# Holding a step until its input is there by the estimate: a re-recorded order for a two-layer hybrid block

## The chip, the cores and the metric

One core of a Trainium2 chip runs the whole program. The metric is the device time of one execution in microseconds (us); what is compared is the median of several runs.

## What is computed

The reference is a block of DEPTH 2 over 256 tokens `x` and 256 context tokens, width 1024, in float32:

```python
def hybrid_layer(x, ctx, sc, sc_ctx, ...):
    shift, scale, gate = jnp.split((sc @ w_ada + b_ada)[:, None, :], 3, axis=-1)
    h = rmsnorm(x, norm_w) * (1.0 + scale) + shift
    aq, ak, av, ag, ao, az, bq, bk, bv, bz, cu, cz, mg = split_cols(h @ w_in)
    ...
    h_a, h_a_c = mlstm_mixer(qa, ka, va, ga, qa_c, ka_c, va_c, ga_c)   # branch A, 4 heads, both directions
    o_b = attend_blocked(qb, ..., lam)                                 # branch B, differential attention
    y_c = fourier_mix(cu) * jax.nn.silu(cz)                            # branch C, fft2
    x = x + gate * merge(y_a, y_b, y_c, mg, w_a_out, w_b_out, w_c_out, w_out)
```

Layer 0 computes tokens and context, layer 1 only the tokens' queries; `merge` gates each branch's output product by a sigmoid and multiplies the sum by `w_out`.

## The kernel before

**Tiles.** Every matmul is made of three products of parts: a float32 operand is split into a hi part (fp32r) and a lo part, its remainder, and hi·hi, hi·lo and lo·hi are summed in PSUM. A weight piece of 512 rows by 256 columns is loaded into `raw`, ScalarE (ACT) copies it to `wh`, and VectorE (DVE) subtracts to make `wl` (`emit_split`, L506, three buffers each). The normalized input, feature-major, is held as `hTh` and `hTl` for the whole layer.

**Two streams of work.** The main stream is the large products with the weights, in chunks of 256 columns (`fm_chunk` L561, `tm_chunk` L587) into the three PSUM banks `pm`. The order of the chunks is a string per layer (ORDER0, ORDER1: A heads, B groups, C groups, merges M, out W). Everything else is side work: the gates of branch A with their scans (`gates_side` L673), the heads (`a_side` L819), attention (`b_side` L986), the Fourier products (`c_side` L1143), the norm of layer 1; it uses five PSUM banks `ps`. Side work is written as generators. After each main step `tick` (L630) continues them, up to about 500 ns of TensorE's time (SIDE_NS) at once, if the time that the generator named by `when(...)` (L186: its tiles written, a bank free, 400 ns on top) has come on an estimated clock.

**What sets the order.** Each engine executes its instructions in the order in which the program emits them. `Clocks` (L91) keeps an estimated time per engine: `book` adds an estimated cost for each instruction, and `Paced` (L127) does so on every call of DVE, ACT, GpSimd (POOL) and SyncE. The estimates only place instructions; a wait on the chip is by semaphores. In this version a step that consists of an ACT and a DVE instruction is emitted whole:

```python
    def split(src, hi, lo, scale=None):
        if scale is None:
            scalar.copy(hi, src)
            vector.tensor_tensor(lo, src, f32(hi), op=ALU.subtract)
```

So DVE's subtract stands in DVE's order right where the ACT copy was emitted, and DVE waits there for ACT.

**The start.** The scale and shift of the norm come from products of `w_ada`, a quarter of the features at a time (`quarter`, L1369). For each quarter: 32 small products of `adaw` on TensorE, `adar` on DVE, 8 tiny products, two `ab` on DVE, then ACT and DVE scale `xT`, ACT casts it to `hTh`, DVE subtracts to `hTl`, for the context tokens and then for the others. Between quarters the first products of head A0 run (table START), on `wh`, `wl` made by `split_to` (L522).

**Names.** In branch A: `gpad` gates before the scans, `lfm`, `Rc`, `Rx`, `at` the scans' tiles, transposed on TensorE by `first` (the identity) and turned into `acol`, `ecol`; `qkh`, `qkl` a head's q and k; `S` their products; `H` the head's output; `Ga` the output gate. In branch B: `kT`, `qT`, `W`, `vt`, and `O`, whose squares `os` go through POOL. L161 is the line of all DVE, ACT and POOL instructions, L232 that of all matmuls, L236 that of transposes.

Of the kernel before, what the change touches and what calls it, by code (L numbers as in the profile page):

```python
# [27 lines left out]
NGEN = 28  # L28
MAINB = 3
# [12 lines left out]
ORDER1 = "A0 B0 A1 B1 A2 A3 C0 B2 B3 M0 C1 C2 C3 M1 M2 W0"  # L42
AHEAD = ((0, 1, 1), (1, 1, 0))
# [47 lines left out]
class Clocks:  # L91
    """When each engine gets to what is emitted, estimated, to place the side work among the main products."""

    def __init__(self):
        self.t = {"pe": 0.0, "dve": 0.0, "act": 0.0, "pool": 0.0, "sync": 0.0}
        self.wrote, self.read, self.ring = {}, {}, {}

    def book(self, engine, outs, ins, cost, tail):
        """an instruction of engine: names of tiles written and read, time held, time until the result is seen"""
# [15 lines left out]

    def rotate(self, tag, bufs, name):
        """the tile called name takes the place of the one bufs before it"""
# [9 lines left out]
class Paced:  # L127
    """An engine whose instructions are booked as they are emitted."""
# [38 lines left out]
def hybrid_kernel(ctx: ExitStack, tc: tile.TileContext, t):  # L167
# [37 lines left out]
    def gen_pair(shape, name):  # L205
        """hi and lo parts, in one slot where they fit"""
# [8 lines left out]
    def ps_main():  # L215
        b = pp.tile([128, 512], F32, tag="pm", name=nm("pm"), bufs=MAINB)
        est.rotate("pm", MAINB, b.name)
        return b

    def ps_side():  # L220
        b = pp.tile([128, 512], F32, tag="ps", name=nm("ps"), bufs=SIDEB)
# [6 lines left out]
    def mm(o, a, b, start, stop):  # L228
        n = int(np.prod(b.shape[1:]))
        ins = [v.name for v in (a, b) if v.name not in ("hTh", "hTl")]  # L230
        est.book("pe", [o.name], ins, max(n * 0.4167 + 2.5, 27) * (4 if b.dtype == F32 else 1) / (128 // o.shape[0]), 160)
        nc.tensor.matmul(out=o, lhsT=a, rhs=b, start=start, stop=stop)  # L232

    def transpose(o, a, idn):
        est.book("pe", [o.name], [a.name], 112, 160)
        nc.tensor.transpose(o, a, idn)  # L236

    def split(src, hi, lo, scale=None):
        if scale is None:
            scalar.copy(hi, src)  # L240
            vector.tensor_tensor(lo, src, f32(hi), op=ALU.subtract)
        else:
            scalar.activation(out=hi, in_=src, func=ACTF.Copy, scale=scale)
            vector.scalar_tensor_tensor(lo, src, scale, f32(hi), op0=ALU.mult, op1=ALU.subtract)

    # ------------------------------------------------------------- constants
# [73 lines left out]
    def rstd_of(ss, n, shape):  # L320
        """(ss / n + eps) ** -0.5 on GpSimd, in place; returns the time at which it is done"""
# [4 lines left out]
    # ------------------------------------------------------------- per-layer small parameters  # L326
# [46 lines left out]
    def ada_rows(l, piece, dma):  # L373
        """w_ada of 512 columns"""
# [8 lines left out]
    def ada_mm(raws, brow, dst):  # L383
        """sc @ w_ada + b_ada: partitions 32 g + stream hold four partial sums"""
# [13 lines left out]
    def ada_finish(l, pc, ks=slice(0, 8)):  # L398
        """pc: shift and scale of some blocks of features"""
# [9 lines left out]
    def ada_gen(l, pieces):  # L409
        """shift and scale columns (pieces 0..3) as a side generator"""  # L410
# [34 lines left out]
    # ------------------------------------------------------------- norm -> feature-major h  # L445
# [3 lines left out]
    def norm_stats(tiles):  # L449
        """normalized copies of some token tiles"""  # L450
# [10 lines left out]
    def norm_apply(l, i, src, base):  # L461
        """src: the normalized transposed blocks base .. base + 3 of token tile i; returns the closing step"""
# [23 lines left out]
    # ------------------------------------------------------------- weight pieces  # L486
# [4 lines left out]
    def emit_raw(i):  # L491
        r = wp.tile([128, 4, 256 + GATES], F32, tag="raw", name=nm("raw"), bufs=RAWB)
# [13 lines left out]
    def emit_split(i):  # L506
        r = made[i]
        n = r.shape[2]
        h = wp.tile([128, 4, 256 + GATES], F32R, tag="wh", name=nm("wh"), bufs=WB)
# [35 lines left out]
    def wcols(w, *cols, form=None):  # L545
        """two pieces of some columns; even features before odd ones along the columns or in pairs of row blocks"""
# [4 lines left out]
    # ------------------------------------------------------------- main-stream products  # L551
# [9 lines left out]
    def fm_chunk(rhs, evac, ntok, bank=ps_main, step=4):  # L561
        """two 128-column blocks of W, feature-major: out[block][128 cols, tokens]"""
# [24 lines left out]
    def tm_chunk(lhs, tiles, evac, single=False, step=4):  # L587
        """256 columns of W, token-major: out[pair][128 tokens, 2, 256]"""
# [24 lines left out]
    # ------------------------------------------------------------- side machinery  # L613
# [4 lines left out]
    def launch(g):  # L618
        rec = {"g": g, "due": 0.0, "done": False}
        side.append(rec)  # L620
        return rec
# [8 lines left out]
    def tick():  # L630
        pe0 = clocks["pe"]
        for rec in list(side[:ACTIVE]):
# [12 lines left out]

    def hrhs(t0, n):
# [7 lines left out]
    # ============================================================= one layer  # L654
# [841 lines left out]
```

## Time and profile before

| what | value |
|---|---|
| runs | 1522.76 us median of 3 (1522.49 to 1524.54) |
| profiled execution | span 1521.1 us from first to last instruction |
| TensorE (PE) | 1499.1 us busy, 99% |
| VectorE (DVE) | 971.5 us, 64% |
| ScalarE (ACT) | 735.0 us, 48% |
| GpSimd (POOL) | 145.7 us, 10% |
| granted TensorE clock | 1.00, mean over the span |

The profile shows one execution, and its span is the time given for it; the median of the runs is 1.66 us above that span. TensorE's matmuls are pipelined: a row's duration (0.28 us for 256 columns) is longer than the distance to the next row's start, so the cadence is read from starts. "Idle" in a bracket is the time between the modelled end of one instruction and the start of the next.

### The profile page before, as it was taken

Reading aid. Unit: us, or ns where it says so; the run is one execution under the profiler, and the core shown is the slowest. Engines: PE = TensorE matmul, PEld = TensorE weight load, DVE = VectorE, ACT = ScalarE, POOL = GpSimd, SP = SyncE. Lnnn points to the kernel's source line nnn. Section 1 sums busy time; section 2 is a strip of 40 time slices with the busy share of each in tenths; the row PEclk is TensorE's granted clock in tenths of the full one; section 3 lists DMA queues with packets and bytes.
Section 4 is the critical chain, followed back from the end, with each engine's and each line's share of the span. In section 5 each row is a group of like instructions: output and inputs, shape, how many; then the busy total and the mean of one; then the engine's idle time right before and its main releaser. Section 6 shows DMA issues by size and latency. Waiting matters only on the chain.

```text
span 1521.1 us, 25867 instructions
## 1 busy us (share of the span) xinstructions
PE 1499.1 (99%) x10410; PEld 1350.8 (89%) x10410; DVE 971.5 (64%) x1833; ACT 735.0 (48%) x1384; POOL 145.7 (10%) x193
## 2 busy tenths in 40 slices
PE   6999999999999999999999999999999999999999
PEld 4888889999998987897786789999999999999998
DVE  3447666677677586436664367677687666977765
ACT  4443556544544545334432235545557554656443
POOL 4001000020100010001024001001020011000200
PEclk9999999999999999999999999999999999999999
DMA  9524333332222222223249337544344523545754
GB/s 310 167 84 127 87 94 105 105 97 70 75 67 69 70 84 70 84 84 97 70 144 337 78 112 228 139 131 133 115 111 118 167 84 109 169 139 153 256 162 151
DMA packets 181611, 192.07 MB, mean 126 GB/s; under 512 B 9818, under 2 KB 174612, under 8 KB 181492
## 3 DMA queue, kind: packets, MB, share of 16 engines
q1 hardware_dynamic: 170080, 159.93, 35.6%
q0 software_dynamic: 7936, 27.27, 5.9%
q10 hardware_dynamic: 3476, 3.23, 0.7%
q8 instruction: 81, 1.33, 0.4%
q14 instruction: 38, 0.31, 0.1%
HBM read 188.23 MB, written 2.17 MB: 125 GB/s over the span
## 4 chain that ended last, share of the span: by engine, by line
PE 92%; DVE 3%; SPq 2%; issue 1%; ACT 1%; DMA 1%; ACTq 0%; DVEq 0%
PE pm L232 76%; PE ps L232 13%; PE ps L236 3%; SPq L161 2%; DVE wl L161 1%; DVE Rx L161 1%; DMA raw<-in_w_in_dram 0%; DVE Rc L161 0%; DMA prow<-in_a_norm_w_dram 0%; DVE lfm L161 0%; DVE at L161 0%; ACT lse L161 0%; DVE Ga L161 0%; ACT wh L161 0%; DVE ntmp L161 0%
## 5 line engine op out<-in xcount | busy, mean ns | idle before, releaser
L161 DVE TENSOR_TENSOR wl<-raw,wh 128x1024 fp32r<-128x1024 f32 x280 | 340.9, 1223 | 193.4 <-ACT wh L161 192.8
L161 ACT CAST wh<-raw 128x1024 fp32r<-128x1024 f32 x280 | 293.6, 1054 | 169.0 <-PE pm L232 135.0
L232 PE MATMUL pm<-hTh,wh 128*128 128x256 f32 (+1 forms) x1008 | 349.0, 346 | 0.0
L232 PE MATMUL pm<-hTl,wh 128*128 128x256 f32 (+1 forms) x1008 | 342.8, 340 | 0.0
L232 PE MATMUL pm<-hTh,wl 128*128 128x256 f32 (+1 forms) x1008 | 342.4, 340 | 0.0
L232 PE MATMUL pm<-wh,hTh 128*128 128x256 f32 (+1 forms) x1152 | 329.8, 286 | 1.5 <-DVE Ga L161 0.8
L232 PE MATMUL pm<-wl,hTh 128*128 128x256 f32 (+1 forms) x1152 | 324.1, 281 | 0.7 <-DVE wl L161 0.7
L232 PE MATMUL pm<-wh,hTl 128*128 128x256 f32 (+1 forms) x1152 | 324.2, 281 | 0.3 <-DVE hTl L161 0.2
L232 PEld LDWEIGHTS pm<-wh,hTh 128*128 128x128 f32 x1152 | 217.3, 189 | 10.4 <-issue 5.5
L232 PEld LDWEIGHTS pm<-wl,hTh 128*128 128x128 f32 x1152 | 216.9, 188 | 2.1 <-DVE wl L161 1.0
L232 PEld LDWEIGHTS pm<-wh,hTl 128*128 128x128 f32 x1152 | 217.5, 189 | 0.7 <-DVE hTl L161 0.7
L232 PEld LDWEIGHTS pm<-hTh,wh 128*128 128x128 f32 x1008 | 189.7, 188 | 30.8 <-issue 9.9
L232 PEld LDWEIGHTS pm<-hTh,wl 128*128 128x128 f32 x1008 | 189.5, 188 | 23.3
L232 PEld LDWEIGHTS pm<-hTl,wh 128*128 128x128 f32 x1008 | 189.7, 188 | 19.0
L232 PE MATMUL pm<-y,wh 128*128 128x512 f32 (+1 forms) x768 | 192.7, 342 | 0.0
L232 PEld LDWEIGHTS pm<-y,wh 128*128 128x128 f32 x768 | 128.9, 188 | 18.3 <-issue 2.6
L232 PE MATMUL pm<-y,wl 128*128 128x512 f32 (+1 forms) x384 | 129.4, 337 | 0.0
L161 ACT ACTIVATE Pt<-ps,mx,qsc 128x512 f32<-128x512 f32 (+1 forms) x96 | 67.1, 706 | 27.7 <-DVE mx L161 22.0
L232 PEld LDWEIGHTS pm<-y,wl 128*128 128x128 f32 x384 | 72.2, 188 | 8.6
L232 PE MATMUL pm<-wh,yf 128*128 128x256 f32 x384 | 73.0, 287 | 0.0
L232 PEld LDWEIGHTS pm<-wh,yf 128*128 128x128 f32 x384 | 59.9, 188 | 0.3
L161 DVE TENSOR_REDUCE mx<-ps 128x1 f32<-128x512 f32 (+1 forms) x96 | 53.0, 593 | 4.3 <-PE ps L232 4.2
(243 smaller groups left out, 1969.8 us busy)
## 6 DMA issues: line engine op xcount, KB each, us to landing
raw<-in_w_in_dram SPq DMA_DIRECT2D x192, 512.0 KB, 3.7
adaw<-in_w_ada_dram POOLq DMA_DIRECT2D x32, 512.0 KB, 7.1
raw<-in_w_out_dram SPq DMA_DIRECT2D x24, 512.0 KB, 4.5
adaw<-in_w_ada_dram SPq DMA_DIRECT2D x16, 512.0 KB, 8.5
raw<-in_w_in_dram SPq DMA_DIRECT2D x32, 256.0 KB, 3.3
raw<-in_w_a_out_dram SPq DMA_DIRECT2D x16, 512.0 KB, 3.4
raw<-in_w_c_out_dram SPq DMA_DIRECT2D x32, 256.0 KB, 3.4
raw<-in_w_b_out_dram SPq DMA_DIRECT2D x16, 512.0 KB, 3.8
```

The costliest lines, as they stand in the source:

```text
L161: return f(*a, **k)
L232: nc.tensor.matmul(out=o, lhsT=a, rhs=b, start=start, stop=stop)
L236: nc.tensor.transpose(o, a, idn)
```

## The change

- `Clocks` gets a list of held steps. `later(src, tiles, fn)` puts a step there with a due time, the estimated time at which its input `src` is written. `elapse` emits due steps ahead of the next DVE or TensorE instruction; `settle` emits a held step when an instruction touches one of its tiles; `clear` does so before a buffer of a ring is reused.
- Held are: the lo part of every `split` (so every `wl`, `hTl` of the start, `qkl`, and the like); in `a_side` the copy of `S` with its masked form `Sd`, and the normalizing `rr`, `H`; the second step of the output gates; in `b_side` the three steps from a product to `O` and its square; in `c_side` the whole split of `T`.
- A matmul's estimated cost becomes its cadence: `max((n * 0.4453 + 4) * (4 if F32), 105)`, times the shares of rows and columns used, where it was `max(n * 0.4167 + 2.5, 27)` times 4 and divided by the row groups; a transpose's 109 where it was 112.
- NGEN, the slots of the general pool, goes from 28 to 30, and the scratch of dynamic DMAs is set to 8192. FLIP_H, FLIP_O, FLIP_K, FLIP_W are False, and the code under them is not reached.

The number of instructions of each engine stays the same. The core of the diff:

```diff
+    def later(self, due, tiles, fn):
+        names = {v.name for v in tiles}
+        for n in names:
+            self.read.setdefault(n, {})["later"] = due + 1200
+        self.held.insert(self.held.index(self.at[-1]) if self.at else len(self.held), (due, names, fn))
...
+    def settle(self, names):
+        while q := next((q for q in self.before() if q[1] & names), None):
+            self.emit_held(q)
+
+    def elapse(self):
+        while not self.at and (q := next((q for q in self.held if q[0] <= max(self.t["pe"], self.t["dve"])), None)):
+            self.emit_held(q)
...
         def call(*a, **k):
+            if self.key == "dve":
+                self.clocks.elapse()
+            self.clocks.settle({v.name for v in list(a) + list(k.values()) if hasattr(v, "shape") and hasattr(v, "name")})
...
     def when(*tiles, banks=1):
...
-        return max([0.0] + [est.wrote[v.name][1] for v in tiles if v.name in est.wrote] + [est.last(n) for n in old]) + READY_NS
+        held = [est.read[v.name]["later"] for v in tiles if "later" in est.read.get(v.name, {})]
+        return max([0.0] + held + [est.wrote[v.name][1] for v in tiles if v.name in est.wrote] +
+                   [est.last(n) for n in old]) + READY_NS
...
     def mm(o, a, b, start, stop):
+        est.elapse()
+        est.settle({o.name, a.name, b.name})
...
-        est.book("pe", [o.name], ins, max(n * 0.4167 + 2.5, 27) * (4 if b.dtype == F32 else 1) / (128 // o.shape[0]), 160)
+        est.book("pe", [o.name], ins, max((n * 0.4453 + 4) * (4 if b.dtype == F32 else 1), 105) * o.shape[0] / 128 * a.shape[0] / 128, 160)
...
     def split(src, hi, lo, scale=None):
+
         if scale is None:
             scalar.copy(hi, src)
-            vector.tensor_tensor(lo, src, f32(hi), op=ALU.subtract)
+            later(hi, (src, lo), lambda: vector.tensor_tensor(lo, src, f32(hi), op=ALU.subtract))
```

Three places of the order follow; names carry buffer numbers, and line 208 of the changed kernel answers to L161, 285 to L232, 291 to L236.

**VectorE in the start**, quarters 0 and 1, from `adar` of quarter 0 on. `wl_66` and `wl_73` are the lo parts of the first two weight pieces. Before:

```order
L161 TENSOR_TENSOR adar_61_246<-ps_57_216,brow_42_163 128x512
L161 TENSOR_TENSOR wl_66_260<-raw_26_127,wh_65_259 128x4x256
L161 COPY ab_71_279<-ps_67_263 128x4
L161 SCALAR_TENSOR_TENSOR ab_71_279<-ps_67_263,pcol_15_105 128x4
L161 TENSOR_SCALAR xT_58_225<-xT_58_225,ab_71_279 128x256
L161 TENSOR_TENSOR hTl_109<-xT_58_225,hTh_108 128x2x256
L161 TENSOR_SCALAR xT_58_225<-xT_58_225,ab_71_279 128x256
L161 TENSOR_TENSOR hTl_109<-xT_58_225,hTh_108 128x2x256
L161 TENSOR_TENSOR wl_73_295<-raw_31_137,wh_72_294 128x4x256
L161 TENSOR_TENSOR adar_80_334<-ps_79_317,brow_42_163 128x512
L161 COPY ab_71_279<-ps_82_349 128x4
L161 SCALAR_TENSOR_TENSOR ab_71_279<-ps_82_349,pcol_15_105 128x4
```

And in the changed kernel, from the second `ab` of quarter 0 on:

```order
L208 SCALAR_TENSOR_TENSOR ab_71_278<-ps_67_262,pcol_15_105 128x4
L208 TENSOR_SCALAR xT_58_225<-xT_58_225,ab_71_278 128x256
L208 TENSOR_TENSOR hTl_109<-xT_58_225,hTh_108 128x2x256
L208 TENSOR_TENSOR wl_66_260<-raw_26_127,wh_65_259 128x4x256
L208 TENSOR_SCALAR xT_58_225<-xT_58_225,ab_71_278 128x256
L208 TENSOR_TENSOR hTl_109<-xT_58_225,hTh_108 128x2x256
L208 TENSOR_TENSOR adar_80_333<-ps_79_316,brow_42_163 128x512
L208 COPY ab_71_278<-ps_82_348 128x4
L208 SCALAR_TENSOR_TENSOR ab_71_278<-ps_82_348,pcol_15_105 128x4
L208 TENSOR_SCALAR xT_62_248<-xT_62_248,ab_71_278 128x256
L208 TENSOR_TENSOR hTl_109<-xT_62_248,hTh_108 128x2x256
L208 TENSOR_TENSOR wl_73_294<-raw_31_137,wh_72_293 128x4x256
```

`wl_66` stood ahead of `ab`, it now stands behind the first `hTl`; `wl_73` stood ahead of `adar` of quarter 1, it now stands behind `ab`, `xT` and the first `hTl` of that quarter. In quarter 3 one `wl` moves in the same way from behind the second `hTl` to ahead of it. TensorE's first 501 rows are in the same order in both.

**ScalarE at the start of layer 1**: `ntmp` and `hTh` are the norm's blocks, `wh` of 1088 columns is a half of the chunk with the gates' columns. Before:

```order
L161 ACTIVATE ntmp_1478_9433<-ps_1477_9428,ab_1302_8298 128x128 x2
L161 CAST hTh_108<-ntmp_1478_9433 128x4x128
L161 ACTIVATE ntmp_1480_9447<-ps_1479_9442,ab_1302_8298 128x128 x2
L161 CAST hTh_108<-ntmp_1480_9447 128x4x128
L161 CAST wh_1482_9456<-raw_1463_9323 128x1088
L161 ACTIVATE ntmp_1485_9468<-ps_1484_9463,ab_1302_8298 128x128 x2
L161 CAST hTh_108<-ntmp_1485_9468 128x4x128
```

Changed:

```order
L208 ACTIVATE ntmp_1478_9430<-ps_1477_9425,ab_1298_8253 128x128 x2
L208 CAST hTh_108<-ntmp_1478_9430 128x4x128
L208 ACTIVATE ntmp_1480_9444<-ps_1479_9439,ab_1298_8253 128x128 x2
L208 CAST hTh_108<-ntmp_1480_9444 128x4x128
L208 ACTIVATE ntmp_1482_9459<-ps_1481_9454,ab_1298_8253 128x128 x2
L208 CAST hTh_108<-ntmp_1482_9459 128x4x128
L208 CAST wh_1484_9468<-raw_1463_9323 128x1088
```

The second `wh` stands behind three blocks of the norm instead of two.

**TensorE at the products S of head A3 in layer 1**, `qkh` and `qkl` being the head's q and k. Before, where the chunk that makes k is `pm_1811` and its last product stands 123 rows ahead of the first row of S:

```order
L232 MATMUL ps_1849_12169<-vl_1703_11210,Ah_1824_11987 128x258
L232 MATMUL ps_1849_12169<-vh_1702_11209,Al_1825_11988 128x258
L232 MATMUL pm_1843_12120<-hTh_108,wh_1829_12003 128x256
L232 MATMUL pm_1843_12120<-hTl_109,wh_1829_12003 128x256
L232 MATMUL pm_1843_12120<-hTh_108,wl_1830_12004 128x256
L232 MATMUL ps_1857_12200<-qkh_1785_11719 128x256
L232 MATMUL ps_1857_12200<-qkl_1786_11720,qkh_1785_11719 128x256
```

Changed, where that chunk is `pm_1841`:

```order
L285 MATMUL pm_1841_12068<-hTh_108,wh_1812_11869 128x512
L285 MATMUL pm_1841_12068<-hTl_109,wh_1812_11869 128x512
L285 MATMUL pm_1841_12068<-hTh_108,wl_1813_11870 128x512
L285 MATMUL pm_1858_12163<-hTh_108,wh_1835_12038 128x256
L285 MATMUL pm_1858_12163<-hTl_109,wh_1835_12038 128x256
L285 MATMUL pm_1858_12163<-hTh_108,wl_1836_12039 128x256
L285 MATMUL ps_1865_12177<-qkh_1801_11788 128x256
L285 MATMUL ps_1865_12177<-qkl_1802_11789,qkh_1801_11788 128x256
```

Three products of the next chunk now lie between k's last product and the first product of S.

## Rows read from the trace of the kernel before

**Rows 1.** The page: busy time of the engines, and the costliest group of VectorE (DVE) with the idle time ahead of it.
```profile
PE 1499.1 (99%) x10410; PEld 1350.8 (89%) x10410; DVE 971.5 (64%) x1833; ACT 735.0 (48%) x1384; POOL 145.7 (10%) x193
...
L161 DVE TENSOR_TENSOR wl<-raw,wh 128x1024 fp32r<-128x1024 f32 x280 | 340.9, 1223 | 193.4 <-ACT wh L161 192.8
```

**Rows 2.** Two stretches of the span: start and end, length, then for PE, PEld, DVE, ACT and POOL the busy us and (x) the instructions, then TensorE's granted clock, the DMA share and GB/s.
```profile
0.00:48.00 48.00, 33.45 (x280) 24.30 (x281) 18.84 (x42) 20.98 (x36) 16.17 (x32) 1.00 1.00 309
...
935.00:1050.00 115.00, 112.06 (x902) 109.49 (x901) 80.42 (x145) 62.37 (x111) 4.30 (x8) 1.00 0.47 136
```

**Rows 3.** The longest wait of TensorE (PE): us in total, times, the longest.
```profile
PE ps L236 <- DMA crow<-in_c_dram: 7.6, 1, 7.6
```

**Rows 4.** The timeline of PE around its waits after 48 us: start, duration, line, operation, output and inputs, and in brackets the idle time ahead of it and what ended it.
```profile
132.37 0.33 PE L236 MATMUL ps<-first,at 64*128 64x64 f32 x2 [0.46 <-DVE at L161]
...
132.88 0.39 PE L232 MATMUL pm<-wh,hTh 128*128 128x256 f32 x1
133.11 0.28 PE L232 MATMUL pm<-wl,hTh 128*128 128x256 f32 x1
...
969.70 0.39 PE L232 MATMUL pm<-wl,hTh 128*128 128x272 f32 x1 [0.74 <-DVE wl L161]
...
975.16 0.39 PE L232 MATMUL pm<-wh,hTh 128*128 128x272 f32 x1 [0.79 <-DVE Ga L161]
...
1020.97 0.38 PE L232 MATMUL ps<-qkh 128*128 128x256 f32 x1 [1.42 <-ACT ecol L161]
```

**Rows 5.** The timeline of DVE in the start, the first two quarters.
```profile
20.09 1.22 DVE L161 TENSOR_TENSOR wl<-raw,wh 128x1024 fp32r<-128x1024 f32 x1
...
23.16 0.69 DVE L161 TENSOR_TENSOR hTl<-xT,hTh 128x512 fp32r<-128x512 f32 x1 [0.93 <-ACT hTh L161]
23.76 0.48 DVE L161 TENSOR_SCALAR xT<-xT,ab 128x256 f32<-128x256 f32 x1
...
30.92 0.16 DVE L161 COPY ab<-ps 128x4 f32<-128x4 f32 x1 [1.21 <-PE ps L232]
...
32.53 0.69 DVE L161 TENSOR_TENSOR hTl<-xT,hTh 128x512 fp32r<-128x512 f32 x1 [0.93 <-ACT hTh L161]
```

**Rows 6.** The timeline of PE in the same stretch.
```profile
23.40 0.28 PE L232 MATMUL pm<-wl,hTh 128*128 128x256 f32 x1
23.90 0.39 PE L232 MATMUL pm<-wh,hTl 128*128 128x256 f32 x1 [0.22 <-DVE hTl L161]
24.12 0.28 PE L232 MATMUL pm<-wh,hTh 128*128 128x256 f32 x1
24.24 0.28 PE L232 MATMUL pm<-wl,hTh 128*128 128x256 f32 x1
...
29.86 1.02 PE L232 MATMUL ps<-first,adar 128*128 128x2 f32 x8 [1.02 <-DVE adar L161]
...
31.29 0.39 PE L232 MATMUL ps<-hTh,wl 128*128 128x512 f32 x1
...
35.13 1.07 PE L232 MATMUL ps<-adaw,sct 128*32 128x256 f32 x16
```

**Rows 7.** The fourth quarter of the start: DVE, then PE.
```profile
53.14 0.69 DVE L161 TENSOR_TENSOR hTl<-xT,hTh 128x512 fp32r<-128x512 f32 x1 [0.74 <-ACT hTh L161]
54.08 1.23 DVE L161 TENSOR_TENSOR wl<-raw,wh 128x1024 fp32r<-128x1024 f32 x1 [0.25 <-ACT wh L161]
...
54.11 0.28 PE L232 MATMUL pm<-wh,hTl 128*128 128x256 f32 x1
```

**Rows 8.** The gates: the transposes of PE that the scans follow (layer 0, layer 1), and DVE's last `at` in either layer, with a `Ga` and a `wl` that stand between in layer 0.
```profile
105.61 0.60 PE L236 MATMUL ps<-first,gpad 128*128 128x128 f32 x4
...
991.49 0.60 PE L236 MATMUL ps<-first,gpad 128*128 128x128 f32 x4
...
126.46 0.69 DVE L161 SCALAR_TENSOR_TENSOR Ga<-Ga,pm 128x512 f32<-128x512 f32 x1
...
130.13 1.22 DVE L161 TENSOR_TENSOR wl<-raw,wh 128x1024 fp32r<-128x1024 f32 x1
...
132.03 0.28 DVE L161 TENSOR_TENSOR at<-pre,Rx 32x128 f32<-32x128 f32 x1
...
1015.38 0.28 DVE L161 TENSOR_TENSOR at<-pre,Rx 32x128 f32<-32x128 f32 x1
```

**Rows 9.** The start of layer 1: on ScalarE (ACT) the first instruction of a block of the norm and the `wh` of 1088 columns behind that block, and DVE's `wl` of it.
```profile
965.04 0.81 ACT L161 ACTIVATE ntmp<-ps,ab 128x128 f32<-128x128 f32 x2
...
967.23 1.10 ACT L161 CAST wh<-raw 128x1088 fp32r<-128x1088 f32 x1
...
968.36 1.29 DVE L161 TENSOR_TENSOR wl<-raw,wh 128x1088 fp32r<-128x1088 f32 x1 [1.15 <-ACT wh L161]
```

**Rows 10.** A head's q and k in layer 1: the last product of the chunk on PE, its hi part on ACT, its lo part on DVE.
```profile
1172.09 0.39 PE L232 MATMUL pm<-hTh,wl 128*128 128x512 f32 x1
...
1173.12 0.59 ACT L161 ACTIVATE qkh<-pm 128x512 fp32r<-128x512 f32 x1
...
1174.25 0.68 DVE L161 SCALAR_TENSOR_TENSOR qkl<-pm,qkh 128x512 fp32r<-128x512 f32 x1
```

**Rows 11.** The end of a group's attention: its last eight products on PE, and the scaled O on DVE.
```profile
453.28 1.03 PE L232 MATMUL ps<-vt,W 128*128 128x256 f32 x8
...
460.22 1.22 DVE L161 TENSOR_TENSOR O<-O,os 128x1024 f32<-128x1024 f32 x1
```

More of the change, by code (lines that the diff above doesn't have):

```diff
@@ L26 @@
 O_CU, O_CZ, O_MG = 8208, 9232, 10256
-NGEN = 28
+NGEN = 30
 MAINB = 3
@@ L96, in __init__, with before, emit_held @@
         self.wrote, self.read, self.ring = {}, {}, {}
+        self.held, self.at = [], []
+    def later(self, due, tiles, fn):
[3 more added lines that the diff above has]
+        self.held.insert(self.held.index(self.at[-1]) if self.at else len(self.held), (due, names, fn))
+    def before(self):
+        return self.held[:self.held.index(self.at[-1])] if self.at else list(self.held)
+    def emit_held(self, q):
+        while q in self.held:
+            p = next(p for p in self.held if p is q or p[1] & q[1])
+            if p is not q:
+                self.emit_held(p)
+                continue
+            i = self.held.index(q)
+            mark = (math.inf, set(), object())
+            self.held[i] = mark
+            for n in q[1]:
+                self.read.get(n, {}).pop("later", None)
+            self.at.append(mark)
+            q[2]()
+            self.at.pop()
+            self.held.remove(mark)
+    def settle(self, names):
[4 more added lines that the diff above has]
+            self.emit_held(q)
     def book(self, engine, outs, ins, cost, tail):
@@ L631, in tick @@
         pe0 = clocks["pe"]
-        for rec in list(side[:ACTIVE]):
+        tails = [r for r in side if r["tail"]]
+        for rec in tails + [r for r in side if not r["tail"]][:ACTIVE]:
             while not rec["done"] and rec["due"] <= clocks["pe"] < pe0 + SIDE_NS and \
@@ L644, in drain, with drain_all @@
                 step(r)
+    def drain_all(states):
+        for s in states:
+            drain([s["rec"]])
+            drain([s["tail"]] if "tail" in s else [])
     def hrhs(t0, n):
@@ L916, in a_side @@
             yield when(H)
-            for dh in range(2):
+            if FLIP_H:
+                s["tail"] = launch(tail(s, "ya", h, H[:, i0:4, :].rearrange("p i (h f) -> p (i h) f", h=2)), True)
+                return
+            for dh in range(0 if FLIP_H else 2):
                 ps = ps_side()
@@ L1096, in b_side @@
                     Pt, ri, at = yield from softmax(hd, i, p2, n)
-                    pend.append((hd, i, Pt, at, n, ri[:, 0:1]))
+                    pend.append([hd, i, Pt, at, n, ri[:, 0:1]])
+                    if FLIP_K and (hd, i) == (0, NTL - 2):
+                        loads[1] = qk_load(1)
+                for p in pend[:-1] if it is not None else pend:
+                    if FLIP_W and not p[3]:
+                        d, Pt = p[2]
+                        yield when(d, banks=0)
+                        flip_in(d, Pt[:, 0, 0:p[4]])
+                        p[2], p[3] = Pt, when(Pt, banks=0)
                 if cur is not None:
@@ L1107, in b_side @@
             yield when(O)
-            for hd in range(2):
+            if FLIP_O:
+                s["tail"] = launch(tail(s, "yb", g, ov), True)
+                return
+            for hd in range(0 if FLIP_O else 2):
                 ps = ps_side()
@@ L1189, in layer, with merge @@
         yacc = {}
-        def merge(recs, ahead, key, first, final):
+        def merge(states, ahead, key, first, final):
             ys = {}
             def split_y(q):
-                ys[q] = gen_pair([128, 2, NTOK], "y")
-                split(ST[key].pop(q), ys[q][0], ys[q][1])
+                yh, yl = ys[q] = gen_pair([128, 2, NTOK], "y")
+                y = ST[key].pop(q)
+                if key == "ya" and FLIP_H:
+                    for u in range(2):
+                        b = 8 * l + 2 * q + u
+                        split(y[:, u, :], yh[:, u, :], yl[:, u, :], scale=awcol[:, b:b + 1])
+                elif key == "yb" and FLIP_O:
+                    split(y, yh, yl, scale=slcol[:, l:l + 1])
+                else:
+                    split(y, yh, yl)
             def spread(g, every):
```

152 lines of the change are left out of this document (119 added, 33 removed).

## The prediction, on record before the changed kernel ran

> **What bounds the kernel now.** I read the page first. TensorE is busy 1499.1 us of a span of 1521.1, and VectorE stands idle 192.8 us ahead of its 280 `wl`, waiting for ScalarE's `wh` [rows 1]. The second number invites this change: an engine with 64% of work spends an eighth of the span at the head of its queue. But TensorE sets the time, so the question is what VectorE's idle time costs TensorE. For that I read the stretches. In the first 48 us TensorE works 33.45 us, and in the stretch around the start of layer 1 it lacks 2.94 of 115 us [rows 2]; elsewhere it is full but for a few tenths and the last stretch, which ends in work that depends on the last product. Then I went through the timeline for every wait of TensorE after 48 us. There are four: 0.46 us for `at`, 0.74 for `wl`, 0.79 for `Ga`, 1.42 for `ecol` [rows 4], 3.4 us in all. Nothing else in the middle can be won by a better order, except the loss at a return from side to main products: after transposes the next product takes from 132.88 to 133.11, 0.23 us [rows 4], where back to back it takes from 24.12 to 24.24, 0.12 us [rows 6]. So the ceiling of the gain is low before any cost is counted, and what is left to ask is which new waits the order brings. I read them from the two orders, place by place, and priced them from rows.
>
> The sum is made against the profiled execution of 1521.1 us; the median of the runs is 1.7 us above it, and I carry that over: 1522.8 is the base.
>
> **The start.** TensorE's order is the same there, VectorE's isn't.
> Quarter 0: `wl` ran at 20.09, before `ab`, in time in which VectorE had nothing else. Now it follows the first `hTl`, which holds VectorE from 23.16 to 23.76 [rows 5]. With 1.22 us for itself it ends at 24.98, and TensorE's product on it starts at about 25.04 where it was 23.40: 1.64 later. 0.22 of waiting for `hTl` right behind goes, and 1.02 of waiting for `adar` at 29.86 [rows 6] goes too, since `adar` no longer stands behind a `wl` and its input is only 1.4 later. Left: +0.2.
> Quarter 1: the second `wl` was done by 29.1, and TensorE used it at 31.29 [rows 6]. Now it stands behind the first `hTl` of the quarter, and that depends on TensorE's own `adar` products by way of `ab`, ACT's `xT` and `hTh`. From `ab` at 30.92 to `hTl` at 32.53 are 1.61 us, `hTl` holds VectorE 0.60, `wl` takes 1.22 [rows 5]: 3.43 after `ab`. With `ab` 0.2 later `wl` ends at 34.55, and TensorE has no other order: it waits 3.1 us at a product that was on time. TensorE was full from 30 to 48, so all of it counts. This is the largest term.
> Quarter 3: a `wl` that waited for ACT at 54.08 now stands ahead of the second `hTl`, which ran at 53.14 [rows 7]. `wl` ends at 55.3, `hTl` at 55.95; TensorE wants it at 54.11 [rows 7]: +1.8.
> Together +5.1. Below, 4.0, if ACT's `wh` or the `xT` of these places run somewhat sooner; above, 6.0. I take 5.1, as each step has a row.
>
> **The gates.** The scans' chain on VectorE runs from the `gpad` transposes at 105.61 to the last `at`, 132.31: 26.7 us, of which one `wl` of 1.22 and four `Ga` of 0.69 leave the interval in the new order: 22.7 [rows 8]. In TensorE's new order the work between both transposes is, at its cadence, 21.4 us where it was 26.0. So the wait is 1.3 and not 0.46: +0.85. In layer 1 the chain is 24.2 us long, 991.49 to 1015.66 [rows 8], and nothing leaves it; TensorE has 21.6 us of work: 2.6, from which I take the 1.42 for `ecol` that lay behind: +1.2. Together +2.0; between 0, if VectorE gets ahead by other held steps, and 3.9, if the wait for `ecol` stays.
>
> **The start of layer 1.** The second `wh` of 1088 columns comes one block of the norm later, 965.04 to 967.23 being one block, 2.2 us, and its `wl` was already late, with TensorE waiting 0.74 [rows 4, 9]. The blocks themselves come about 0.4 sooner. The `wl` is 1.8 later, and the wait of 0.79 for `Ga` is then covered: +1.0, between 0 and 2.2.
>
> **Heads in layer 1.** S of A3 follows three products behind k's last product; its second product, which reads the lo part, comes 0.7 us after it. From that product at 1172.09 the lo part was there at 1174.93, 2.8 us later, of which ACT was busy elsewhere for about 1 [rows 10]. So TensorE waits 1.1 to 2.1; in A2, with 2.15 us of lead, 0 to 0.65. I take 1.6 for both. Before, the leads were over 8 us.
>
> **Ends of groups and heads.** From the last product at about 454.06 to O scaled at 461.44 are 7.4 us [rows 11]. Three groups of layer 0 have 5.4, 5.4 and 5.6 us of TensorE's work there in the new order, over 9 before. If the chain stays as long, that costs 5.8; if VectorE takes the scaling 2 us sooner, nothing. The chain of H has the same form, and might cost as much again. I take 2.5, ends 0 and 10: nearer to the low end, since `O` waits in these 7.4 us behind other work of VectorE, and side work is spread thinner now.
>
> **Returns.** The new order has 293 returns from side to main products, 23 fewer than 316; at 0.11 each at most 2.5 us, at least nothing, since after S products a return loses nothing. I take −1.0.
>
> The lo parts elsewhere, the slots, the DMA scratch and the branches under the FLIP names cost nothing: the first have cover of several microseconds of TensorE's work, the rest changes no instruction. If that cover went, the price is one ScalarE and one VectorE instruction each, 2.8 us as above.
>
> **Sum:** 5.1 + 2.0 + 1.0 + 1.6 + 2.5 − 1.0 = +11.2, so 1534.0 us. By the ends of the terms, +2.6 to +24.6; its own likely range is 1528 to 1541.
>
> **A rule against it.** Granted clock is 1.00 in the first 48 us, although TensorE waited 7.6 us in one piece there and was busy 33.45 of 48 [rows 2, 3]. The Trainium skill, "TensorE: Matmul & The Clock Gate", section "HAM oscillation — how this bites in real kernels", says that a long enough gap of TensorE between bursts makes the clock fall, and that products behind it then run at half speed. This trace doesn't agree so far: the longest wait shows no lower clock. Were it so behind the new wait in quarter 1, the products from there to the next `adaw` group, 3.8 us, would take twice as long.
>
> **Rivals.**
> - The gain arrives and nothing is paid: the four waits (3.4) and all 23 returns (2.5) go, 1522.8 − 5.9 = 1516.9. It is decided at one point, whether the second `wl` is there when TensorE gets to it near 31.3 us. For it: 193 us of VectorE's idle time are freed. Against it: the order puts that `wl` behind a chain that begins at 30.92. 6%.
> - It comes out even: the start costs 5.1, the four waits and the returns give 5.9 back, 1522.0; or the change does not reach TensorE, 1522.8. For it: 99% busy. Against it: the leads that shrink. 14%.
> - Only the start costs; the shorter leads elsewhere suffice and returns give 1: 1522.8 + 5.1 − 1.0 = 1526.9. 18%.
> - All shortened chains take as long as they did: by the upper ends +24.6, 1547.4. Against it: VectorE's waiting goes, so they should get shorter. 10%.
> - The clock falls behind the wait in quarter 1 and stays down for those 3.8 us: 1537.8. 4%.
> My forecast has 48%.
>
> **Chances.** About 0.2%, 3 us, can be told from no change. Faster by more: the first rival, 0.06. Within it: the second, 0.14. Slower: 0.80. The range from 1522 to 1541 leaves out the first rival and the fourth, 16%.
>
> **What would show it.** Right: a wait of about 3 us for `wl` near 31 to 35 us, one of 1.8 for `hTl` near 58, the waits for `at` of 1 to 3 us, one for `wl` of 2 to 3 us at the start of layer 1, new waits for `qkl` in layer 1 and for `O`. TensorE busy unchanged within 3 us, VectorE's idle time ahead of `wl` well below 193 us. Wrong: a start as long as before, or a middle of the program that gets shorter by more than 6 us, which no row of before offers.

## The result, and the profile of the changed kernel

The changed kernel takes 1545.53 us (median of 4, 1544.3 to 1546.88) against 1522.62 us, a ratio of 1.0148, interval 1.0134 to 1.0162: 22.9 us slower. The forecast was slower by 11, in a range up to 1541; the direction holds, the size doesn't. The profiled execution has a span of 1542.5 us, 21.4 above [rows 1]'s 1521.1.

The page of the changed kernel, busy time of the engines (line 285 answers to L232, 291 to L236, 208 to L161):

```profile
PE 1507.5 (98%) x10410; PEld 1353.9 (88%) x10410; DVE 965.3 (63%) x1833; ACT 734.1 (48%) x1384; POOL 154.0 (10%) x193
```

TensorE is busy 8.4 us more with the same instructions and idle 13.0 more. VectorE's idle time ahead of `wl` fell only from 193 to 184 us. Both are against the prediction's signs, which were a TensorE busy time unchanged within 3 us and a VectorE idle time well below 193. What TensorE waited for, us in total, times, the longest:

```profile
PE pm L285 <- DVE wl L208: 4.0, 4, 1.5
PE ps L291 <- DVE at L208: 3.1, 2, 2.0
PE pm L285 <- ACT wh L208: 3.0, 2, 1.6
PE ps L285 <- DVE wl L208: 3.0, 1, 3.0
...
PE pm L285 <- DVE hTl L208: 1.7, 1, 1.7
PE ps L285 <- DVE Al L208: 1.0, 2, 0.6
```

Comparing the start of the n-th main product in both traces says where the time went, since both kernels make the same 8,208 main products in the same order. The changed kernel is 9.75 us behind by the 150th (80 us of its own span), 13.1 from the end of layer 0's side work on, and 21.5 at the last. So 9.7 us are lost in the start, 3.4 in the rest of layer 0, 8.3 in layer 1.

**The start.** VectorE's rows, start and duration in us, with the idle time ahead and what ended it:

```profile
23.81 0.69 DVE L208 TENSOR_TENSOR hTl<-xT,hTh 128x512 fp32r<-128x512 f32 x1 [0.86 <-ACT hTh L208]
24.42 1.22 DVE L208 TENSOR_TENSOR wl<-raw,wh 128x1024 fp32r<-128x1024 f32 x1
...
35.76 0.69 DVE L208 TENSOR_TENSOR hTl<-xT,hTh 128x512 fp32r<-128x512 f32 x1 [0.86 <-ACT hTh L208]
36.38 1.22 DVE L208 TENSOR_TENSOR wl<-raw,wh 128x1024 fp32r<-128x1024 f32 x1
...
61.86 1.23 DVE L208 TENSOR_TENSOR wl<-raw,wh 128x1024 fp32r<-128x1024 f32 x1 [1.69 <-ACT wh L208]
63.00 0.68 DVE L208 TENSOR_TENSOR hTl<-xT,hTh 128x512 fp32r<-128x512 f32 x1
```

`wl` follows the first `hTl` in quarters 0 and 1 and precedes the second in quarter 3, as the order said. TensorE in the same stretch:

```profile
25.69 0.58 PE L285 MATMUL pm<-wl,hTh 128*128 128x256 f32 x1 [1.48 <-DVE wl L208]
26.07 0.42 PE L285 MATMUL pm<-wh,hTl 128*128 128x256 f32 x1
26.29 0.41 PE L285 MATMUL pm<-wh,hTh 128*128 128x256 f32 x1
...
28.34 3.38 PE L285 MATMUL ps<-adaw,sct 128*32 128x256 f32 x32
31.65 0.39 PE L285 MATMUL pm<-wh,hTh 128*128 128x256 f32 x1
...
32.00 0.28 PE L285 MATMUL pm<-wh,hTl 128*128 128x256 f32 x1
32.11 0.28 PE L285 MATMUL pm<-wh,hTh 128*128 128x256 f32 x1
...
37.65 0.50 PE L285 MATMUL ps<-hTh,wl 128*128 128x512 f32 x1 [2.95 <-DVE wl L208]
...
38.67 0.63 PE L285 MATMUL ps<-hTh,wl 128*128 128x512 f32 x1
39.10 0.63 PE L285 MATMUL ps<-hTh,wh 128*128 128x512 f32 x1
```

The waits are there (1.48, 2.95, and 1.69 for `hTl` at 63.74), but something else is too. Behind the first wait, products of 256 columns start 0.22 us apart instead of 0.12, and the 32 products of `adaw` take 3.3 us instead of the 1.9 of before; behind the second, products of 512 columns start 0.43 apart instead of 0.23. That is half speed, and the granted clock says so (stretches of 2 us: length, busy time of PE, PEld, DVE, ACT, POOL, then the granted clock, DMA share, GB/s):

```profile
24.00:26.00 2.00, 0.52 (x2) 0.32 (x3) 1.96 (x3) 0.28 (x1) 0.33 (x1) 0.63 1.09 326
26.00:28.00 2.00, 2.00 (x11) 2.00 (x10) 0.69 (x1) 1.95 (x4) 0.00 (x0) 0.50 1.40 323
...
38.00:40.00 2.00, 2.00 (x7) 1.53 (x6) 0.69 (x1) 1.57 (x2) 0.00 (x0) 0.54 1.10 345
...
42.00:44.00 2.00, 2.00 (x27) 1.55 (x29) 0.00 (x0) 0.00 (x0) 0.00 (x0) 1.00 1.00 313
```

0.50 is the lower level of 1.2 GHz, 1.00 is 2.4 GHz. TensorE had waited before each fall; whether the wait made the clock fall is taken up with e1 and e3. The two stretches cost 4.0 us: 2.5 from 26.1 to 31.7, 1.5 from 38.2 to 41.2, counted as each product's distance above its distance at full speed.

**The middle.** The waits that answer to [rows 4], and new ones:

```profile
136.78 0.34 PE L291 MATMUL ps<-first,at 64*128 64x64 f32 x2 [1.08 <-DVE at L208]
...
984.28 0.39 PE L285 MATMUL pm<-wh,hTh 128*128 128x272 f32 x1 [1.36 <-ACT wh L208]
985.60 0.39 PE L285 MATMUL pm<-wl,hTh 128*128 128x272 f32 x1 [0.94 <-DVE wl L208]
...
1028.78 0.33 PE L291 MATMUL ps<-first,at 64*128 64x64 f32 x2 [2.03 <-DVE at L208]
...
1090.11 0.39 PE L285 MATMUL pm<-wh,hTh 128*128 128x256 f32 x1 [1.64 <-ACT wh L208]
1091.37 0.39 PE L285 MATMUL pm<-wl,hTh 128*128 128x256 f32 x1 [0.87 <-DVE wl L208]
...
1203.37 0.39 PE L285 MATMUL ps<-qkh 128*128 128x256 f32 x1 [0.34 <-ACT qkh L208]
1204.09 0.39 PE L285 MATMUL ps<-qkh,qkl 128*128 128x256 f32 x1 [0.22 <-DVE qkl L208]
```

Those for `at`, for `wh` and `wl` at the start of layer 1 and for `qkh`, `qkl` were forecast. The two near 1090 weren't. This is POOL and ACT ahead of them:

```profile
1079.77 1.64 POOL L208 TENSOR_TENSOR bst<-bst,chalf 128x8 f32<-128x8 f32 x1
1081.35 1.18 POOL L208 DMA_DIRECT2D Rb<-dR  x2
...
1086.06 1.60 ACT L208 ACTIVATE Rb<-Rb,acol 128x256 f32<-128x256 f32 x4 [5.96 <-DMA Rb<-dR]
...
1089.02 1.98 ACT L208 CAST wh<-raw 128x1024 fp32r<-128x1024 f32 x2
```

`Rb` are a head's rows of decay exponents, loaded by a DMA from POOL's queue. POOL worked on attention's `bst` until 1081.4 and only then issued the DMA. ScalarE stood 5.96 us at the head of its queue for it, and the `wh` that TensorE needed at 1088.5 stood behind. In the kernel before no such wait was above 0.51 us; in the changed one three are (2.1, 2.9, 6.0).

### The profile page after: what moved, and what is told of

Same layout as the page of the kernel before. It is cut to its first block, busy times and chain, and to the rows that moved or that the text cites. A ratio compares the mean times of both kernels' runs of the same rounds, so it can differ in the third digit from the quotient of the medians.

```text
span 1542.5 us, 25874 instructions
## 1 busy us (share of the span) xinstructions
PE 1507.5 (98%) x10410; PEld 1353.9 (88%) x10410; DVE 965.3 (63%) x1833; ACT 734.1 (48%) x1384; POOL 154.0 (10%) x193
## 4 chain that ended last, share of the span: by engine, by line
PE 84%; DVE 7%; ACT 4%; issue 2%; DMA 1%; SPq 1%; POOL 0%; ACTq 0%; DVEq 0%; POOLq 0%
PE pm L285 69%; PE ps L285 12%; PE ps L291 3%; DVE wl L208 2%; ACT Rb L208 2%; SPq L208 1%; DVE Rb L208 1%; DVE Rx L208 1%; ACT wh L208 1%; DVE Al L208 1%; DMA adaw<-in_w_ada_dram 1%; DMA Rb<-dR 1%; POOL bst L208 0%; DVE Ga L208 0%; DMA prow<-in_subln_w_dram 0%
```

## Experiments

All are compared with the kernel before, which ran beside them on the same chip. With both parts of the change taken out of the changed kernel, every engine has the order of the kernel before row for row; so what is left of the change (30 slots, the DMA scratch, code that isn't reached) moves no instruction.

**e1, the start unheld.**
```diff
     def later(src, tiles, fn):
-        est.later(ready(src), (src,) + tuple(tiles), fn)
+        if holding[0]:
+            est.later(ready(src), (src,) + tuple(tiles), fn)
+        else:
+            fn()
...
+        holding[0] = q == 3
```


> The changed kernel, but until the fourth quarter of the start is done every step is emitted at once, as before; from there on steps are held as in the changed kernel. TensorE's order is that of the changed kernel row for row, and VectorE's differs from it in three places of the start alone. Theory A (the place of three wl and what follows from it cost the start 9 us: the waits of 1.5, 3.0 and 1.7 us, and products that run at half the speed behind the first two): about 1545.5 - 9.1 = 1536.4, span with a granted clock of 1.00 throughout. Rival B (only the waits count, the clock would have fallen in any case): 1545.5 - 5.1 = 1540.4. Rival C (the start's loss is slack that later waits take back): within 2 us of 1545.5.

1539.85 us, ratio 1.0106 (1.0091 to 1.0122): 5.7 us less than the changed kernel, which is Rival B's number and not mine. The start's three waits are gone, and the profile is 1.6 us behind by 72 us instead of 9.75. Its clock is not up throughout, as Theory A had it: the products of the start run at half speed until 29 us although none of the new waits is there, and layer 1 has three stretches at half speed, of 1.5, 1.05 and 1.5 us at 977, 1023 and 1087, behind waits that the changed kernel's profile has too, there without a fall.

So Rival B's reason, that the clock would have been low in any case, holds for a part of the start. Nine more profiles have a start without the new waits (the kernel before and e4 to e11). In e4, e6, e9 and e11 the clock falls between 24.4 and 25.0 us, where it falls in the changed kernel, and in e7 and e10 it is low until 29 us, as in e1; only in the kernel before, e5 and e8 is the stretch from 22 to 30 us at full speed. These are TensorE's rows of e4, whose waits are those of the kernel before, and its stretches of 2 us:

```profile
23.69 0.38 PE L285 MATMUL pm<-wh,hTh 128*128 128x256 f32 x1 [0.74 <-ACT hTh L208]
...
24.41 0.58 PE L285 MATMUL pm<-wh,hTl 128*128 128x256 f32 x1 [0.23 <-DVE hTl L208]
24.79 0.41 PE L285 MATMUL pm<-wh,hTh 128*128 128x256 f32 x1
...
24.00:26.00 2.00, 1.77 (x9) 1.59 (x8) 1.26 (x3) 1.37 (x4) 0.13 (x1) 0.60 1.24 312
26.00:28.00 2.00, 2.00 (x21) 1.22 (x23) 0.12 (x1) 2.00 (x4) 0.00 (x0) 0.54 1.02 283
```

The changed kernel's first stretch at half speed (2.5 us) can therefore not be put down as a whole to its wait of 1.48. It lasts until 31.3 us there and until 27.8 to 28.4 in those four; that the wait prolonged it is possible and not shown. The seven are only 0.5 to 1.6 us behind the kernel before by 80 us (e5 and e8: 0.3 and 0.7), and TensorE's wait of 1.02 for `adar` [rows 6] is gone in them. The second fall, behind the wait of 2.95, is in no profile without that wait. The two stretches of layer 1 in this kernel's profile, same columns:

```profile
950.00:1060.00 110.00, 104.63 (x804) 101.74 (x805) 73.56 (x131) 56.79 (x99) 4.30 (x8) 0.97 0.46 132
1060.00:1270.00 210.00, 206.46 (x1651) 198.24 (x1650) 150.33 (x326) 119.34 (x243) 25.35 (x27) 0.99 0.39 113
```

So in layer 1 TensorE's clock fell behind a wait of 1 to 2 us in one execution and not in another, and I can't sum it place by place.

**e2, the kernel before with the start held.** As e1 with `holding[0] = q != 3` and the old costs.

> The kernel before, with the holding of steps in the start alone (up to the fourth quarter), old costs, nothing held afterwards: its order is that of the kernel before except for the same three places of VectorE. Theory A: 1522.6 + 9.1 to 9.7 = about 1532. Rival B (waits alone): about 1527.7. Rival C: within 2 us of 1522.6.

1532.0 us, ratio 1.005 (1.0038 to 1.0063): +9.0 in the median, Theory A. The five executions are not alike, though: three take 1532.0 to 1532.7, two take 1528.6 and 1529.1, within 1.5 us of Rival B. The profile is of the longest. The start's waits there are 1.28, 2.95 and 1.68 us, and the distance to the kernel before is 10.7 us by 81 us and 9.9 at the end: hardly anything takes it back. In this profile the loss is 3.7 us more in idle rows, about 4 of half speed behind the waits, and 1.3 of half speed that lies ahead of the first wait: the clock is low until 32.6 us, as it is in e1 until 29. So the three moved instructions cost 6 to 10 us an execution, and how much of that a low clock adds differs from one to the next.

**e3, the waits filled.**
```diff
         nc.tensor.matmul(out=o, lhsT=a, rhs=b, start=start, stop=stop)
+        if o.name[:2] == "pm" and "main" not in filled:
+            filled.add("main")
+            fill(a, b, 12)
+        elif o.name[:2] == "ps" and b.name.startswith("hTl") and "side" not in filled:
+            filled.add("side")
+            fill(a, b, 13)
```


> The changed kernel with added products in the two long waits of the start, written to a bank that nobody reads: 12 products of 256 columns behind the first product on wh in quarter 0, 13 of 512 columns behind the second product of the waiting group in quarter 1. They fit into the waits (12 x 0.118 = 1.4 us and 13 x 0.232 = 3.0 us) and leave every other order as it is. Theory A (the clock fell because TensorE was idle): the granted clock stays at 1.00 and some 4.4 us come back, 1541.1. Rival (the clock falls for another reason, or the half speed is a matter of the operands): no gain, 1545.5 to 1546.

1542.34 us, ratio 1.0122 (1.0108 to 1.0136): 3.2 us less than the changed kernel with 25 more products in it. In its stretches that answer to those of the changed kernel above the clock stays up:

```profile
24.00:26.00 2.00, 1.95 (x16) 1.74 (x15) 1.26 (x3) 0.70 (x2) 0.17 (x1) 1.00 1.12 326
26.00:28.00 2.00, 2.00 (x35) 1.25 (x35) 0.65 (x1) 2.00 (x5) 0.00 (x0) 1.00 1.33 320
...
38.00:40.00 2.00, 2.00 (x35) 1.08 (x34) 0.00 (x0) 0.00 (x0) 0.00 (x0) 1.00 1.10 341
```

With the clock up, the start of this profile is 4.9 us behind the kernel before by 81 us, where the changed kernel's is 9.75: at full speed the waits cost about what the sum gave them. For the second place this shows the cause: the clock fell right behind the wait of 2.95 us in both profiles that have it unfilled (the changed kernel and e2), not where it was filled, and in none without it. For the first place it doesn't, since the clock falls or is low there in seven profiles whose start never had the wait. The median gave back 3.2 and not 4.4; this profile has two stretches of 1.5 us at half speed in layer 1, at 982 and 1026, which the changed kernel's has not.

**e4, holding alone, after the start.** As e1, with the old costs.

> The changed kernel with the old estimated costs of matmul and transpose, and nothing held in the start: what holding alone does after the start. Compared with the run with the start unheld (1539.9), which has holding and the new costs, and loses 16.9 us against the kernel before. Theory D (both halves of the change shorten leads, each at its own places): by the order the second wh at the start of layer 1 stands where it stood before, but S in two heads of layer 1 follows k's last product by 0.9 and 1.2 us, where a lo part takes 1.8 to 2.8: 1522.8 + 5 to 9, about 1530. Rival E (the new costs alone shorten the leads, holding only matters in the start): within 2 us of 1522.8. Rival F (holding alone does it): about 1539.

1527.97 us, ratio 1.0029 (1.0017 to 1.004): +4.3. Its new waits of TensorE are 2.06 and 0.22 us for `qkh` and `qkl` near 1185 and six of 0.2 to 0.7. This is below what Theory D gave and far from Rival F.

**e5, the new costs alone.**
```diff
     def later(src, tiles, fn):
-        est.later(ready(src), (src,) + tuple(tiles), fn)
+        fn()
```


> The changed kernel with nothing held anywhere: the new estimated costs of TensorE alone. Its start is that of the kernel before. By the order the second wh of the gates' piece stands behind all four blocks of the norm at the start of layer 1, two blocks of 2.2 us later than before: a wait of about 4 to 5 us for wl there; S stays over 3 us behind k, and O is down to 5.6 us at one group. Theory D: 1522.8 + 5 to 9, about 1530, most of it at that one place. Rival E (costs alone): about 1539. Rival F: within 2 us of 1522.8.

1537.91 us, ratio 1.0093 (1.0079 to 1.0107): +14.2, close to Rival E. The estimate of TensorE's cadence does most of the loss after the start, with nothing held. At the start of layer 1:

```profile
972.51 0.39 PE L285 MATMUL pm<-wh,hTh 128*128 128x272 f32 x1 [3.20 <-ACT wh L208]
973.83 0.39 PE L285 MATMUL pm<-wl,hTh 128*128 128x272 f32 x1 [0.94 <-DVE wl L208]
```

`wh` stands behind four blocks of the norm. The wait for `Rb` at the head of ScalarE's queue is there as well (4.2 us at 1075), with TensorE's waits of 2.33 and 0.87 behind it, and two stretches at half speed of 1.5 us follow these places.

**e6, the rows awaited.** As e1, and in a head's weighing:
```diff
+                yield when(R)
                 for st, t0, w, o in parts:
                     scalar.activation(out=R[:, o:o + w], in_=R[:, o:o + w], func=ACTF.Relu, scale=-1.0,
```


> The changed kernel with the start unheld, and one more yield: a head's weighing is continued only when its rows Rb have landed by the estimate, so that ScalarE does not take its Relu before. In the changed kernel ScalarE stood 6.0 us ahead of that Relu near 1086 us, 2.9 near 1035 and 2.1 near 221, for the DMA of Rb, with the next wh behind it. Theory G (this wait at the head of ScalarE's queue makes wh late near 1090): the waits of 2.0 and 0.9 us there and the half speed behind them go, and the time is 1539.9 - 3 to 5, about 1536. Rival (wh would be late anyway, since it waits for TensorE to free its buffer): within 1.5 us of 1539.9.

1531.75 us, ratio 1.0048 (1.0036 to 1.0061): 8.1 less than e1, more than Theory G said (the kernel before took 0.7 us more beside this run than beside e1). ScalarE has no idle time above 0.5 us ahead of `Rb` any more, and the waits of 1.99 and 0.88 near 1086 are gone, with the half speed behind them. So are those of 0.5 to 0.6 for `Ah` and `Al` near 230 and 273 and one of 0.45 near 1052, which I had not counted as hanging on it. One of 1.25 for `W` near 1127 is new. Of the 8.7 us between the two profiles, idle time of TensorE after 48 us gives 4.1 and the stretch at half speed about 1.5; the rest I did not assign, and the yield moves other side work as well.

**e7 to e9, the level of the costs.** As e5, with TensorE's costs times 0.925, 0.89 and 1.04.
```diff
-        est.book("pe", [o.name], ins, max((n * 0.4453 + 4) * ..., 105) * o.shape[0] / 128 * a.shape[0] / 128, 160)
+        est.book("pe", [o.name], ins, 0.925 * max((n * 0.4453 + 4) * ..., 105) * o.shape[0] / 128 * a.shape[0] / 128, 160)
```


> The kernel with the new estimated costs alone, nothing held (1537.9), but all of TensorE's costs times 0.925, about the level of the old ones for 256 and 512 columns (0.4453 x 0.925 = 0.412 ns a column, old 0.4167). Theory M (the old costs ran 8% short of TensorE's real cadence, so that a due time came that much later in real time, a margin on every lead; the new ones take it away): the order has its leads back, 24.9 us from gpad to the last at, 7.1 for O, the second wh two blocks into the norm; within 3 us of the kernel before, 1521 to 1526. Rival N (the form of the new costs does it, the floor and the shares of rows for small products, not the level): still 1534 to 1540.

> The same with costs times 0.89, a margin larger than before's. By the order gpad to the last at has 26.0 and 27.7 us, more than in the kernel before (24.9, 25.6), S is 29 us behind k, O at 7.0 and more; but the second wh is three blocks into the norm instead of two, and side work is later. Theory M: the waits for at and ecol of before (0.5 and 1.4 us) go, one wait of about 1.5 to 2.5 us for wl comes at the start of layer 1; 1521 to 1526, around the kernel before. Rival N: 1534 to 1540.

> The same with costs times 1.04, no margin at all: leads of 21.0 us for at, 2.7 for S, 5.4 for O, the second wh behind all four blocks. Theory M: worse than with the costs as they are, by the further 1.8 us at the gates and by waits for S and O: 1540 to 1546. Rival N: as with the costs as they are, 1536 to 1540.

0.925: 1539.0 us, ratio 1.0105 (1.009 to 1.012). 0.89: 1552.06, 1.019 (1.0175 to 1.0205). 1.04: 1538.74, 1.0103 (1.0086 to 1.012). Theory M as I had put it fell: 0.925 was to be the kernel before again. The timeline of TensorE with 0.925 says why, with its waits for `at`, `wl`, `Ga`, `ecol`, and then two of the last ones:

```profile
133.83 0.34 PE L291 MATMUL ps<-first,at 64*128 64x64 f32 x2 [0.47 <-DVE at L208]
...
972.94 0.39 PE L285 MATMUL pm<-wl,hTh 128*128 128x272 f32 x1 [0.73 <-DVE wl L208]
978.40 0.39 PE L285 MATMUL pm<-wh,hTh 128*128 128x272 f32 x1 [0.79 <-DVE Ga L208]
...
1024.21 0.38 PE L285 MATMUL ps<-qkh 128*128 128x256 f32 x1 [1.43 <-ACT ecol L208]
...
1418.03 0.38 PE L285 MATMUL ps<-vt,W 128*128 128x256 f32 x1 [1.30 <-ACT W L208]
...
1431.71 1.09 PE L291 MATMUL ps<-first,Q 128*128 128x128 f32 x4 [3.47 <-DVE Q L208]
```

Up to 1400 us the waits in the layers are, to 0.02 us, the four of [rows 4], and one of 1.25 near 470. The loss comes after that. Side work was now so late that attention's last tiles were emitted with no main product left to put between them; from 1400 to 1440 us TensorE is busy 32.4 us of 40 at a mean clock of 0.83. With 0.89 the piece that stands alone is 9.9 us long by the order, and the loss is larger.

**e10, the costs times 0.96.**

> The kernel with the new estimated costs alone, nothing held, all of TensorE's costs times 0.96. With 0.925 the waits up to 1400 us were those of the kernel before again, and the loss came at the end, where side work was so late that 3.9 us of it stood alone in TensorE's order, with waits on its own chain; with 0.96 no such piece stands alone by the order. Theory M in its second form (the level is a throttle with two sides: too high takes the leads away, too low leaves side work for the end): no waits near 1420, and between the leads of 0.925 and 1.0: 23.5 us at the gates, O at 7.0, the second wh three blocks into the norm; 1525 to 1531. Rival N (the form of the costs does it): 1534 to 1540.

1527.51 us, ratio 1.0029 (1.0019 to 1.004), as the second form says, and not as Rival N. Over the five levels the times are 1552.1 (0.89), 1539.0 (0.925), 1527.5 (0.96), 1537.9 (1.0) and 1538.7 (1.04): a lowest point between two losses. Each level is one order, and levels near 0.96 weren't tried, so where the lowest point lies is known no better than that. 1.04 was no worse than 1.0, against Theory M, which had said 1540 to 1546.

**e11, holding after the start with the old costs, q, k and the rows awaited.** As e4, with e6's yield and one ahead of the products S:
```diff
+            yield when(qkh, qkl)
             for j in range(4):
                 ps = ps_side()
```


> Holding after the start alone, with the old costs (1528.0), and two more yields in a head: before its products S, until q and k are split, and before its weighing, until Rb has landed. The waits that holding alone left are 2.1 and 0.2 us for qkh and qkl near 1185, 3.3 us of ScalarE's for Rb near 1021 and some of 0.2 to 0.5 for wl. Theory D (S too close behind k, Rb at the head of ScalarE's queue): these go, 1522 to 1526, as the kernel before. Rival (they come back elsewhere, since H then follows 6.4 us behind its products): 1527 to 1530.

1521.35 us, ratio 0.9987 (0.9978 to 0.9996): 6.6 less than e4, and 2 us less than the kernel before. TensorE's waits, in the form of [rows 3]:

```profile
PE pm L285 <- DVE wl L208: 1.4, 2, 0.7
PE pm L285 <- DVE Ga L208: 0.8, 1, 0.8
```

Of the waits of [rows 4], those for `at` and `ecol` are gone and those for `wl` and `Ga` remain; one of 0.67 for `wl` near 945 is new, and none for q and k is left. It is the only version that is faster than the kernel before, and by little.

## Why the prediction was right and wrong

**Right.** That no more than 6 us could be won, by [rows 4] and the returns, and that the start's order costs more than that. The waits of the start were forecast at 1.64, 3.1 and 1.8 and measured 1.48, 2.95 and 1.69, and with the clock up they cost 4.9 us in all (e3), where the sum had 5.1. The waits for `at` (1.3 and 2.6 forecast, 1.08 and 2.03 measured), for the second `wh` of the norm and for q and k came where the order put them.

**Wrong: the clock in the start's sum.** The failing step is the rule that I set against the trace and gave 4%: the sum counts waits at full speed and puts a lower clock at nothing. [rows 2, 3] show a clock of 1.00 although TensorE waited 7.6 us, and I took that as evidence that a wait doesn't lower it. It was evidence of nothing. In e1 and e2 products run at half speed from about 19 us on while the stretches there still say 1.00: before its first change in an execution the record doesn't show the lower level, so the stretch in which TensorE waits for `crow` can't tell. The trace of the kernel before had this in it as well. Ahead of 20 us, 16 products of `adaw` take

```profile
17.48 1.94 PE L232 MATMUL ps<-adaw,sct 128*32 128x256 f32 x16
```

and at 35.13 the same 16 take 1.07 [rows 6], under the same clock of 1.00. The start's term was 5.1 and measured 9.0 in the median (e2; 5.6 to 9.8 by execution). The difference is half speed, but not all of it hangs on the new waits: behind the wait of 2.95 it does (e3), in the stretch from 24.5 us a low clock is there in seven of ten profiles without the wait. The rule of the Trainium skill, "TensorE: Matmul & The Clock Gate", section "HAM oscillation — how this bites in real kernels", that products behind a long enough gap of TensorE run at half speed, agrees with the changed kernel's rows behind the wait of 2.95 (0.43 us apart instead of 0.23) and with e3.

**Wrong: ScalarE's queue.** The sum has no term for a DMA behind POOL. I had counted what TensorE waits for along its own leads (products to split, scans to transposes), and not what stands at the head of ScalarE's queue when side work comes sooner. Waiting for `Rb` gave back 8.1 us (e6), with all that hangs on it and whatever else the yield moved: the largest single error.

**Wrong size.** Ends of groups and heads, +2.5 forecast: TensorE has no wait for `O` or `H` at all in the changed kernel; `Ah` and `Al` took 1.5, by way of `Rb` as e6 shows. Gates +2.0: the waits grew by 1.2. Heads in layer 1 +1.6: 0.6. Start of layer 1 +1.0: 0.8. The returns' −1.0 I can't find in the traces. Three slips of the sum decide nothing: in quarter 0, 1.64 − 0.22 − 1.02 leaves 0.4 and not 0.2; the gates' upper end is 3.45 and not 3.9, since 0.46 of it was there before; and the upper ends as they stand add up to 24.85, not 24.6.

**What the terms belong to.** I priced places and did not ask which part of the change moved them. Holding costs 9.0 in the start (e2) and 4.3 after it (e4); the estimate alone costs 14.2 (e5); after the start both together cost 16.9 (e1). The estimate's part is a matter of level: a due time is compared with TensorE's estimated clock, and before, that clock advanced some 8% less for a product of 256 columns than TensorE does (0.4167 x 256 + 2.5 = 109 ns, where the starts stand 118 apart), which made every lead that much longer in real time. With the true cadence the leads have no reserve (e5), with still lower costs side work is left over at the end (e7, e8). That a better level lies between is shown by e10; that the reserve is all there is to the difference between e10 and the kernel before (4 us) isn't.

**Open.** Of the 21.4 us between the profiles, the idle rows from 20 us on account for 12.6 and half speed for 4.0; the first product behind each of ten more waits loses 0.1, and the rest, about 3.8, is spread over small distances that I did not assign. Why the clock fell behind a wait in e1 and not behind the same wait in the changed kernel wasn't tried, nor why it is low from 24.5 us in some executions of a start without the new waits and not in others.

## What to carry to other kernels

When an order comes from an estimated clock, its errors are part of the tuning: making the estimate true takes away a reserve that nobody had written down, so put the reserve where it is needed (wait for the split, wait for the load) before correcting the clock. In a changed order look for each engine at what now stands at the head of its queue waiting for another, transfers included, and not only at the busy engine's own leads. A wait of TensorE can cost more than its length, by half speed behind it: the start's waits cost 4.9 us where the clock stayed up (e3) and 9.75 where it did not. Before half speed is put down to a wait, look whether profiles without the wait show it too.

## What the runs showed of the hardware

The granted clock of a stretch can read 1.00 while products run at half speed, if no change of the clock was recorded before it: 0.21 us for 256 columns in e1 (24.6 to 27.8 us) and e2, and in the kernel before 16 products of `adaw` in 1.94 us at 17.48 against 1.07 at 35.13. The distance of starts is the surer reading. A wait of 2.95 us was followed by 3 us at half speed in both profiles that have it (the changed kernel and e2), and not where 13 added products filled it (e3). Half speed from 24.5 us on was there in the changed kernel with a wait of 1.48 us, and in four kernels with none above 0.74 (e4, e6, e9, e11). In layer 1 waits of 0.9 to 2.0 us were followed by 1.0 to 1.5 us of loss in some executions and by none in others.
